# A hybrid decoder step on one core: final states, gate product, memsets and two stages of the RWKV part placed elsewhere in the order

## The chip, the cores and the metric

The kernel runs on one core of a Trainium2 chip. Five engines of the core matter here, and each runs its own instructions in order: PE (TensorE: matrix products and transposes; its weight loads are listed apart as PEld), DVE (VectorE), ACT (ScalarE), POOL (GpSimd) and SP (SyncE, which in this kernel only issues DMAs). PE writes to PSUM, which has 8 banks per partition; DVE and ACT read PSUM, POOL works in SBUF. The metric is device time in microseconds (us), the median of the runs shown; less is better.

## What is computed

One inference step of one layer, for a prompt of 512 rows and 8 samples of 8 new rows each, so 576 rows in all. The normalised input goes through one wide projection. Two branches then run side by side, RWKV-7 time mixing and differential attention; sigmoid gates merge them, and a squared-ReLU MLP with a final norm follows. The part that the change touches is the RWKV branch:

```python
def rwkv7_branch(Pr, S0, lp):
    r, k, v, wd, ad, gd = jnp.split(Pr, RWKV_SPLITS, axis=-1)
    w = -jax.nn.softplus(-(lp['w0'] + jnp.tanh(wd) @ lp['w2']).astype(f32)) - 0.5
    decay = jnp.exp(-jnp.exp(w))
    a = jax.nn.sigmoid((lp['a0'] + ad @ lp['a2']).astype(f32))
    g = jax.nn.sigmoid(gd) @ lp['g2']
    ...
    kk = kk / jnp.maximum(jnp.linalg.norm(kk, axis=-1, keepdims=True), 1e-12)
    k = k.astype(f32) * (1.0 + (a - 1.0) * lp['k_a'].astype(f32))
    S, y = rwkv7_scan(S0, hs(r), hs(decay), hs(k), hs(v), -kk, kk * hs(a))
    mean = jnp.mean(y, axis=-1, keepdims=True)
    var = jnp.mean(jnp.square(y - mean), axis=-1, keepdims=True)
    y = (y - mean) * lax.rsqrt(var + GN_EPS) * ln_x_w + ln_x_b
    bonus = jnp.sum(hs(r) * hs(k) * lp['r_k'], axis=-1, keepdims=True) * hs(v)
    o = (y + bonus).reshape(B, T, W_A).astype(Pr.dtype) * g
    return o, S
```

The state S, one 64 x 64 matrix per head, is an output too, for the prompt and for each sample.

## The kernel before

Data lie transposed: features on the 128 partitions, the 576 rows along the free axis. The recurrence is done in chunks of 64 rows: 8 chunks of the prompt, and a ninth that holds the 8 samples. The 8 RWKV heads go in four head pairs, hp 0 to 3; the two heads of a pair (`par` 0 and 1) share the partitions, 64 each.

**Dense products.** Every large projection is a generator (`stream`, L154): it loads a weight tile, ACT and DVE split it into a high and a low half (`halve`), and it then yields one matmul after another, 288 columns each. `waiting` is a list of such generators: `zs` and `shifted` (ps_z, the RWKV inputs), `gate` (ps_g) and `branch_b` (ps_brb). `take(n)` (L216) puts the next n of their matmuls at this place of the program; `fill(n)` (L224) does the same and also ties them behind the last matmul issued so far (`issue_after` gives an order on one engine, not a wait). The rest of the kernel's PE time between 190 and 525 us is the chunked recurrence, made of small products, with dense ones between them.

**The planner.** The program is not issued as written. A planner orders the instructions of each engine: of those that it holds for ready it takes the one that stands first in the program (or has a priority of its own, `prio`). So a later instruction may go ahead of an earlier one that still waits for data or for a buffer. Once the order is made, each engine keeps it, whatever the true times are.

**Buffers.** `bank(name)` gives one of three PSUM banks in turn ("w"); `tbank` and `cbank(0, ...)`, `cbank(1, ...)` give one bank each, used by the solves of stage 3, by the chain, and later by the MLP. In SBUF, the tag "G" has three tiles, shared by nb, vm, y2 and oa; a fourth tile waits until one of the three has been read for the last time.

**Stages of one head pair.** `rwkv(hp)` (L742) is a generator too, cut by `yield` into stages:

1. Norms and masks (L752 to L836): squares of k, column sums pn, the norm by a power on POOL (nr, L760), its spread to 640 columns (nb, L763), the transposes pk of nb, decays (u, cum, pe, pinv), kk, the bonus product pbn from rkp, the stacked tiles KB and ST, and the masked products pA. POOL sets the unused half of each ST to zero (L818).
2. Keys and states (L840 to L872): the transposes pV into SVU and pK into KBt, the load of the samples' states s0, and their products pI.
3. The solves (L876 to L926): eight steps pW/pZ, with 9 dense products tied behind each, and the tile TT.
4. Final states of the samples (L929 to L941): two masked copies vm on POOL, four matmuls pF, two DVE operations on sn, a store issued by POOL.
5. Mean and variance of the outputs (L944 to L955): DVE and ACT, with the tile y2 and a power on POOL (`rpow`, L240 to L243).
6. Outputs (L958 to L976): y times the power, transposes pTy, copies into oa by ACT, scale, bonus, then the gate product pg in two halves, each multiplied into oa. For hp 2 and 3, `split` (L983) makes the high and low halves (oab) for the branch product; hp 0 and 1 are stored to memory and loaded again later (L1078).

`chain(pr)` (L987) runs the nine chunks in order for two head pairs at once; it needs stages 1 to 3 of both and makes their y. `run(*stages)` (L1045) advances each named head pair by one stage. The list of calls from L1051 to L1081 is the order of the whole part:

```python
    run(0, 0)
    take(221)
    run(0, 1, 1)
    take(106)
    run(1)
    chain(0)
```

After `chain(1)` come `take(226)`, the final states of hp 2 and 3, their means and variances, and then for each of them 47 dense products and the outputs. What is left of the dense list follows (`take(2001)`), then the branch products ps_bra (L1101), which read oab of all four head pairs, and the output projection ps_wo.

Of the kernel before, what the change touches and what calls it, by code (L numbers as in the profile page):

```python
# [8 lines left out]
F32 = mybir.dt.float32  # L9
# [6 lines left out]
P = 128  # L16
# [3 lines left out]
NB = 8  # L20
# [16 lines left out]
C_ID, C_OB, C_M, C_MS, C_LM, C_I32, C_HS, C_SEL, C_MB, C_CM, C_END = (  # L37
    0, 128, 256, 384, 512, 672, 704, 706, 738, 746, 748)
# [3 lines left out]
def tile_hybrid_step(ctx, tc, xT, xsT, ktab, vtab, s0T, ptab, w_in, vecs, w2a2, g2, lamv,  # L42
                     w_bra, w_brb, w_out, w_up, w_down, cst, bias_p, bias_s,
                     yT, kTo, vTo, Sp, Ss, sh):
    nc = tc.nc
    PE, VE, AE, GE = nc.tensor, nc.vector, nc.scalar, nc.gpsimd
    PS = bass.MemoryType.PSUM

    def pool(name, bufs=1, stack=ctx, **kw):
        return stack.enter_context(tc.tile_pool(name=name, bufs=bufs, **kw))  # L50
# [6 lines left out]
    def act(out, in_, func=AF.Copy, **kw):  # L57
        ring["act"] = AE.activation(out=out, in_=in_, func=func, **kw)  # L58

    def tt(out, a, b, op, eng=None):  # L60
        ins = (eng or VE).tensor_tensor(out=out, in0=a, in1=b, op=op)  # L61
        if eng is None:
            ring["tt"] = ins

    def stt(out, a, s, b, op0, op1):
        VE.scalar_tensor_tensor(out=out, in0=a, scalar=s, in1=b, op0=op0, op1=op1)
# [4 lines left out]
    def mm(out, lhsT, rhs, start=True, stop=True):  # L71
        ring["mm"] = PE.matmul(out=out, lhsT=lhsT, rhs=rhs, start=start, stop=stop)  # L72
        return ring["mm"]
# [17 lines left out]
    MUL, ADD, SUB, MAX = ALU.mult, ALU.add, ALU.subtract, ALU.max  # L91
# [9 lines left out]
    def bank(name):  # L101
        return psw.tile([P, 512], F32, tag="w", name=name)

    def tbank(name):
        return psc.tile([P, 512], F32, tag="t", name=name)

    def cbank(i, name):
        return (psy if i else psc).tile([P, 512], F32, tag=f"c{i}", name=name)
# [3 lines left out]
    c = const.tile([P, C_END], F32, name="cst_sb")  # L112
# [103 lines left out]
    def take(n):  # L216

        while waiting and n:
            if next(waiting[0], None) is None:
                waiting.pop(0)  # L220
            else:
                n -= 1

    def fill(n):  # L224

        with tc.issue_after(ring["mm"].ins):
            take(n)
# [43 lines left out]
    with tc.tile_pool(name="xin", bufs=2, reuse_waits="tile") as xin:  # L271
# [6 lines left out]
        for k in range(0, KT, 4):  # L278
            for j in range(3):
                with prio(FEED + 1000 + 10 * k + j):  # L280
                    name = f"raw_{'qkv'[j]}0_{k}"
                    if k == 0:
                        raw = ring["pool"].tile([P, 4, P], F32, tag="raw", name=name, bufs=3)
                    else:
                        raw = zw.tile([P, 1 + NX], F32, tag="z" if j else "tz", name=name,
                                      bufs=2 if j else 1)[:, :4 * P].rearrange("p (k w) -> p k w", k=4)
# [378 lines left out]
    for h in range(HB):  # L665
        if h:
            qkv(h)
        for cc in range(2):
            GE.tensor_copy(
                out=qbd[64 * cc:64 * cc + 64, :, h, 8 * cc:8 * cc + 8],  # L670
                in_=qT[64 * cc:64 * cc + 64, h, NPR:].rearrange("p (b q) -> p b q", b=NB))
# [45 lines left out]
    rt = pool("rt", 2, stack=rk, reuse_waits="tile")  # L717

    def ch(a):
        return a.rearrange("p (c t) -> p c t", t=64)  # L720

    def m3(ap_, n):
        q, w = ap_.shape
        return ap_.rearrange("p (o w) -> p o w", o=1).broadcast_to([q, n, w])
# [14 lines left out]
    pair = {}  # L739
    halves = [(par, slice(64 * par, 64 * par + 64)) for par in range(2)]  # L740

    def rwkv(hp):  # L742
        e = hp % 2
        own = pair.setdefault(hp // 2, {})
# [3 lines left out]
        def tmp(tag, bufs=1):  # L748
            return rt.tile([P, NT], F32, tag="T", name=f"{tag}_{hp}", bufs=6)
# [5 lines left out]
        for t, o in enumerate(toks):  # L755
            mm(pn[:, 2 * t:2 * t + 2], sq[:, o:o + P], c[:, C_HS:C_HS + 2])
        (fill if hp != 2 else take)(8)
        nr = stat.tile([P, 10], F32, tag="nr", name=f"nr{hp}")
# [1 line left out]
        GE.tensor_tensor(out=nr, in0=nr, in1=mhalf[:, :10], op=ALU.pow)  # L760

        nb = rt.tile([P, 5, P], F32, tag="G", name=f"nb{hp}", bufs=3)
        GE.tensor_copy(out=nb.rearrange("p t (a d) -> p (t a) d", a=2),  # L763
                       in_=nr.rearrange("p (a o) -> p a o", o=1).broadcast_to([P, 10, 64]))
        u = tmp("u")
        aa = tmp("aa")
        for t0, n in HALF:
# [12 lines left out]
        pc = rb_.tile([P, 16], F32, tag="pc", name=f"pc{hp}", bufs=4)  # L780
# [33 lines left out]
        for par, rows in halves:  # L814
            stt(KB[rows, :, par], ch(aa)[rows], 0.5, ch(pinv)[rows], MUL, MUL)
            tt(KB[rows, :, 1 - par], ch(k2)[rows], ch(pinv)[rows], MUL)
            st = rb_.tile([P, NCH, 2, 64], F32, tag=f"ST{par}", name=f"ST{par}_{hp}")
            GE.memset(st[64 - 64 * par:128 - 64 * par], 0.0)  # L818
            stt(st[rows, :, 0], ch(kk)[rows], -1.0, ch(pm)[rows], MUL, MUL)
            tt(st[rows, :, 1], ch(r)[rows], ch(pe)[rows], MUL)  # L820
            ST.append(st)
# [4 lines left out]
        for par in range(2):  # L826
            rows = slice(64 * par, 64 * par + 64)
# [14 lines left out]
        SVU = own["SVU"][:, :, e]  # L842
        for cs, pV in two_chunks(f"pV{hp}", vv):
            for a, c0, c1 in cs:
                src = pV[64 * a:64 * a + 64].rearrange("p (c w) -> p c w", w=P)[:, :(c1 - c0 + 1) // 2]
                act(SVU[64:128, c0:c1:2, 0], src[:, :, 0:64])
                act(SVU[0:64, c0:c1:2, 1], src[:, :, 64:128])
        if hp >= 2:
            fill(8)
        KBt = rb_.tile([P, NCH, 2, 64], F32, tag="KBt", name=f"KBt{hp}")  # L850
        for c0, cn in ((0, 4), (4, 4), (8, 1)):
# [5 lines left out]

        s0 = rt.tile([P, NB, 64], F32, tag="s0", name=f"s0_{hp}")
        nc.sync.dma_start(out=s0, in_=s0T[hp])
        (fill if hp == 3 else take)(8)  # L860
        pI = bank(f"pI{hp}")
        for b in range(NB):
            for par, rows in halves:
# [2 lines left out]
        for par in range(2):  # L866
            rows = slice(64 * par, 64 * par + 64)
# [57 lines left out]

        own[e] = ST, KBt, TT, ABR, pc  # L926
        yield

        pF = bank(f"pF{hp}")  # L929
        vms = []  # L930
        for par in range(2):
            vm = rt.tile([P, NB, 64], F32, tag="G", bufs=3, name=f"vm{hp}{par}")
            tt(vm, m3(SVU[:, 8, par], NB),
               c[:, C_MB:C_MB + NB].rearrange("p (b o) -> p b o", o=1).broadcast_to([P, NB, 64]), MUL, GE)
            vms.append(vm)
        for par, rows in halves:
            mm(pF[rows], KBt[:, 8, par], vms[par].rearrange("p b i -> p (b i)"))
        sn = s0
        tt(sn, s0, pF.rearrange("p (b i) -> p b i", b=NB), ADD)
        tt(sn, sn, pc[:, 8:16].rearrange("p (b o) -> p b o", o=1).broadcast_to([P, NB, 64]), MUL)  # L940
        nc.gpsimd.dma_start(out=Ss[hp], in_=sn)  # L941

        yield
        y = own["y"][:, e]  # L944

        mean = stat.tile([P, NCH], F32, tag="mean", name=f"mean{hp}")
# [20 lines left out]
        ts(oa, oa, v(V_LW + hp), MUL, v(V_LB + hp), ADD)  # L967
        tt(oa, oa, bv, ADD)
        for t0, n in HALF:
            pg = bank(f"pg{hp}{t0}")  # L970
            mm(pg[:, :n], wg[:, hs], sg[:, t0:t0 + n])
            tt(oa[:, t0:t0 + n], oa[:, t0:t0 + n], pg[:, :n], MUL)
            if hp >= 2:
                split(oab[hp], oa, t0, n)
        if hp < 2:
            nc.gpsimd.dma_start(out=oa_d[hp], in_=oa)  # L976

    oab = [None] * 4

    def half_rows(hp):  # L980
        oab[hp] = rb_.tile([P, 2, NT], F32R, tag=f"ST{hp % 2}", name=f"oab{hp}")

    def split(dst, src, t0, n):  # L983
        act(dst[:, 0, t0:t0 + n], src[:, t0:t0 + n])
        tt(dst[:, 1, t0:t0 + n], src[:, t0:t0 + n], f32(dst[:, 0, t0:t0 + n]), SUB)
# [55 lines left out]


    gens = [rwkv(hp) for hp in range(4)]

    def run(*stages):  # L1045
        for hp in stages:
            while Pt[8 + hp] is None:
                take(2)
            next(gens[hp], None)
# [3 lines left out]
    waiting += ga[:5]  # L1053
    run(0, 0)
    take(221)
    run(0, 1, 1)
    take(106)
    run(1)
    chain(0)
    run(2, 0, 1)  # L1060
    take(190)
# [6 lines left out]
    run(0, 1)  # L1068
    chain(1)
    take(226)  # L1070
    run(2, 3, 2, 3)
    for hp in range(2, 4):
        with tc.issue_after(ring["mm"].ins):
            take(47)
            run(hp)
    for hp in range(2):
        o_ = rt.tile([P, NT], F32, tag="T", name=f"oa{hp}", bufs=6)
        nc.sync.dma_start(out=o_, in_=oa_d[hp])  # L1078
        half_rows(hp)
        split(oab[hp], o_, 0, NT)  # L1080
# [216 lines left out]
    rows = []  # L1297
    for d, n in enumerate((None, "t1", "b11", "t2", "b21", "t3", "b22", "t4")):
        if n:
            t = fp.tile([P, 2, 4, 288], F32R, tag=f"h_{n}", name=f"w3_{d}", bufs=1)  # L1300
            t = t.rearrange("p i k t -> p (i k t)")
# [5 lines left out]
    for t0, n in LAST:  # L1307
# [47 lines left out]
        for d in range(KT):  # L1355
# [4 lines left out]
            if d + 1 in ends:  # L1360
                i = ends.index(d + 1)
# [119 lines left out]
```

## Time and profile before

| what | us |
|---|---|
| median of 3 runs | 1008.45 (1007.78 to 1008.55) |
| the profiled execution | 1010.31 |
| its span, first to last instruction | 1008.5 |
| PE busy | 977.0 |
| DVE busy | 692.2 |
| ACT busy | 496.6 |
| POOL busy | 99.3 |

The profile is of one execution; all its times count from the start of the span. A row of the timeline has start, duration, engine, line, operation, output and inputs, shapes, and in brackets the idle time of the engine before it with what ended it. Many helpers record their operations at one line (L61, L66, L69 on DVE, L58 on ACT, L72 and L76 on PE, L150 for weight loads), so the name of the tile tells which operation it is. Matmul durations overlap, since the next one starts before the last has ended; the distance of two starts is what a matmul costs. The granted clock of PE is 1.00 at full speed; its mean over the span is 0.990.

### The profile page before, as it was taken

To read this page: it belongs to the slowest core of one execution; us is meant where nothing else is said; L and a number is where in the kernel's file an instruction comes from. 1 tells how busy PE (TensorE), PEld (TensorE's weight loads), DVE (VectorE), ACT (ScalarE), POOL (GpSimd) and SP (SyncE) were. 2 spreads that over 40 slices of the span, in tenths; PEclk is the share of its full clock that TensorE was granted. 3 is DMA by queue.
4 is the path that set the end of the run, shared out by engine and by line. 5 is a ranking of instruction groups with operands and counts; after the bars stand their busy time and mean duration, and the time that the engine had idled before them with its cause. 6 is when DMAs were issued, how large, how long until landed. Compare 5 with 4: busy or idle time off the path is not lost.

```text
span 1008.5 us, 24415 instructions
## 1 busy us (share of the span) xinstructions
PE 977.0 (97%) x10012; PEld 920.4 (91%) x10012; DVE 692.2 (69%) x1445; ACT 496.6 (49%) x1086; POOL 99.3 (10%) x179
## 2 busy tenths in 40 slices
PE   9999999899999998999989999999999999999996
PEld 9999998898888887988879999999999999999996
DVE  6698666864937679454569888966666666666744
ACT  6576555344435354453334656644444444444732
POOL 2511001301010430000210120000000000000001
PEclk9999999999989999999999999999999999999998
DMA  7322673121121135323366632222222222221402
GB/s 266 138 66 88 203 223 120 50 65 45 43 68 45 59 109 156 97 80 113 102 203 203 211 121 87 88 90 90 89 85 92 86 85 84 85 84 43 134 3 94
DMA packets 50833, 105.75 MB, mean 105 GB/s; under 512 B 6066, under 2 KB 8114, under 8 KB 50594
## 3 DMA queue, kind: packets, MB, share of 16 engines
q1 hardware_dynamic: 47442, 96.95, 30.0%
q0 software_dynamic: 1648, 5.35, 1.5%
q8 instruction: 79, 1.29, 0.6%
q10 hardware_dynamic: 1632, 1.89, 0.5%
q14 instruction: 32, 0.26, 0.1%
HBM read 89.38 MB, written 14.78 MB: 103 GB/s over the span
## 4 chain that ended last, share of the span: by engine, by line
PE 81%; DVE 8%; ACT 5%; issue 3%; POOL 1%; DMA 1%; DVEq 0%; SPq 0%; POOLq 0%; ACTq 0%
PE ps_dn L72 20%; PE ps_g L72 9%; PE ps_z L72 8%; PE ua L1217 5%; PE ux L1217 5%; PE ps_k L72 3%; PE ps_bra L72 2%; PE uc L1217 2%; PE ud L1217 2%; PE ub L1217 2%; PE ps_q L72 2%; PE pch L72 2%; PE ps_brb L72 2%; PE ps_v L72 2%; PE pA L72 2%
## 5 line engine op out<-in xcount | busy, mean ns | idle before, releaser
L72 PE MATMUL ps_dn<-q,hi_dn 128*128 128x288 f32 x768 | 154.8, 296 | 0.0
L72 PEld LDWEIGHTS ps_dn<-q,hi_dn 128*128 128x128 f32 x768 | 122.8, 188 | 1.4
L72 PE MATMUL ps_dn<-q,lo_dn 128*128 128x288 f32 x384 | 113.2, 295 | 0.0
L72 PE MATMUL ps_g<-xl,hi_g 128*128 128x288 f32 x256 | 80.0, 313 | 0.0
L72 PE MATMUL ps_g<-xh,lo_g 128*128 128x288 f32 x256 | 79.3, 310 | 0.7 <-issue 0.7
L72 PE MATMUL ps_g<-xh,hi_g 128*128 128x288 f32 x256 | 79.4, 310 | 0.0
L72 PEld LDWEIGHTS ps_dn<-q,lo_dn 128*128 128x128 f32 x384 | 72.0, 188 | 0.0
L72 PE MATMUL ps_z<-xh,lo_z 128*128 128x288 f32 (+1 forms) x224 | 68.9, 308 | 0.0
L72 PE MATMUL ps_z<-xh,hi_z 128*128 128x288 f32 (+1 forms) x224 | 67.6, 302 | 0.0
L72 PE MATMUL ps_z<-xl,hi_z 128*128 128x288 f32 (+1 forms) x224 | 66.9, 298 | 0.0
L61 DVE TENSOR_TENSOR ya<-ya,ps_dn 128x288 f32<-128x288 f32 x96 | 43.4, 452 | 29.4 <-PE ps_dn L72 29.4
L58 ACT ACTIVATE hi_dn<-raw_dn 128x512 fp32r<-128x512 f32 x48 | 30.1, 627 | 56.1 <-PE ps_dn L72 56.1
L1217 PE MATMUL ua<-h_b,hi 128*128 128x288 f32 x256 | 53.3, 298 | 0.9 <-ACT p L58 0.9
L72 PEld LDWEIGHTS ps_g<-xh,hi_g 128*128 128x128 f32 x256 | 49.0, 191 | 3.8 <-issue 2.6
L1217 PE MATMUL ux<-h_t,hi 128*128 128x288 f32 x256 | 52.3, 296 | 0.0
L58 ACT ACTIVATE c<-c 128x288 f32<-128x288 f32 x112 | 48.5, 439 | 6.5 <-DVE c L61 4.9
L72 PEld LDWEIGHTS ps_g<-xl,hi_g 128*128 128x128 f32 x256 | 48.9, 191 | 1.9
L72 PEld LDWEIGHTS ps_g<-xh,lo_g 128*128 128x128 f32 x256 | 48.9, 191 | 1.6 <-DVE lo_g L61 0.2
L58 ACT ACTIVATE hi<-a 128x1024 fp32r<-128x1024 f32 (+1 forms) x32 | 27.0, 845 | 43.0 <-PE ps_dn L72 34.9
L61 DVE TENSOR_TENSOR lo<-s,hi 128x1024 fp32r<-128x1024 f32 x32 | 39.2, 1225 | 10.5 <-ACT hi L58 10.4
L72 PE MATMUL ps_dn<-q,w 128*128 128x320 f32 (+1 forms) x336 | 46.3, 297 | 0.0
L72 PEld LDWEIGHTS ps_dn<-q,w 128*128 128x128 f32 x336 | 45.2, 190 | 0.1
(399 smaller groups left out, 2816.9 us busy)
## 6 DMA issues: line engine op xcount, KB each, us to landing
a<-in_w_up_dram SPq DMA_DIRECT2D x32, 512.0 KB, 3.3
raw_dn<-in_w_down_dram SPq DMA_DIRECT2D x64, 256.0 KB, 2.9
raw_g<-in_w_in_dram SPq DMA_DIRECT2D x32, 256.0 KB, 3.1
raw_z<-in_w_in_dram SPq DMA_DIRECT2D x28, 256.0 KB, 2.9
gt_d<-gg SPq DMA_DIRECT2D x16, 288.0 KB, 2.4
g<-gt_d SPq DMA_DIRECT2D x16, 288.0 KB, 3.5
kp<-in_ktab_dram SPq DMA_DIRECT2D x16, 256.0 KB, 3.9
vp<-in_vtab_dram SPq DMA_DIRECT2D x16, 256.0 KB, 3.5
```

The costliest lines, as they stand in the source:

```text
L58: ring["act"] = AE.activation(out=out, in_=in_, func=func, **kw)
L61: ins = (eng or VE).tensor_tensor(out=out, in0=a, in1=b, op=op)
L72: ring["mm"] = PE.matmul(out=out, lhsT=lhsT, rhs=rhs, start=start, stop=stop)
L1217: ring["mm"] = PE.matmul(out=ps[:, :288], lhsT=l[:, k], rhs=hb[blk][:, h, k], start=start and i == 0, stop=i == 11, skip_group_check=skip)
```

## The change

Four edits, all of order or place; the arithmetic is the same.

- The final states become a function. hp 0 and 1 call it where stage 4 was; for hp 2 and 3 it becomes the last stage, behind the outputs.
- The gate product pg of hp 2 and 3 uses `tbank` and `cbank(0)` for its two halves, not two of the three "w" banks.
- The memsets of ST are tied, on POOL, behind the spread of the norm (nb) of the same head pair.
- Stage 2 of hp 1 comes behind `take(106)`, with 8 dense products tied behind its pV (new) and 8 tied behind its pK (before: 8, not tied).

```diff
+    def final_states(hp, SVU, KBt, s0, pc):
+
+        pF = bank(f"pF{hp}")
+        vms = []
+        for par in range(2):
+            vm = rt.tile([P, NB, 64], F32, tag="G", bufs=3, name=f"vm{hp}{par}")
+            tt(vm, m3(SVU[:, 8, par], NB),
+               c[:, C_MB:C_MB + NB].rearrange("p (b o) -> p b o", o=1).broadcast_to([P, NB, 64]), MUL, GE)
+            vms.append(vm)
+        for par, rows in halves:
+            mm(pF[rows], KBt[:, 8, par], vms[par].rearrange("p b i -> p (b i)"))
+        sn = s0
+        tt(sn, s0, pF.rearrange("p (b i) -> p b i", b=NB), ADD)
+        tt(sn, sn, pc[:, 8:16].rearrange("p (b o) -> p b o", o=1).broadcast_to([P, NB, 64]), MUL)
+        nc.gpsimd.dma_start(out=Ss[hp], in_=sn)
+
     def rwkv(hp):
...
-        GE.tensor_copy(out=nb.rearrange("p t (a d) -> p (t a) d", a=2),
-                       in_=nr.rearrange("p (a o) -> p a o", o=1).broadcast_to([P, 10, 64]))
+        spread_ = GE.tensor_copy(out=nb.rearrange("p t (a d) -> p (t a) d", a=2),
+                                 in_=nr.rearrange("p (a o) -> p a o", o=1).broadcast_to([P, 10, 64]))
...
-            GE.memset(st[64 - 64 * par:128 - 64 * par], 0.0)
+            with tc.issue_after(spread_.ins):
+                GE.memset(st[64 - 64 * par:128 - 64 * par], 0.0)
...
-        if hp >= 2:
+        if hp >= 1:
             fill(8)
...
-        (fill if hp == 3 else take)(8)
+        (fill if hp % 2 else take)(8)
...
         own[e] = ST, KBt, TT, ABR, pc
         yield
-
-        pF = bank(f"pF{hp}")
...
-        nc.gpsimd.dma_start(out=Ss[hp], in_=sn)
-
-        yield
+        if hp < 2:
+            final_states(hp, SVU, KBt, s0, pc)
+            yield
         y = own["y"][:, e]
...
         for t0, n in HALF:
-            pg = bank(f"pg{hp}{t0}")
+
+            pg = bank(f"pg{hp}{t0}") if hp < 2 else cbank(0, f"pg{hp}{t0}") if t0 else tbank(f"pg{hp}{t0}")
             mm(pg[:, :n], wg[:, hs], sg[:, t0:t0 + n])
...
         if hp < 2:
             nc.gpsimd.dma_start(out=oa_d[hp], in_=oa)
+        else:
+            yield
+            final_states(hp, SVU, KBt, s0, pc)
...
     take(221)
-    run(0, 1, 1)
+    run(0, 1)
     take(106)
-    run(1)
+    run(1, 1)
     chain(0)
...
     take(226)
-    run(2, 3, 2, 3)
+    run(2, 3)
     for hp in range(2, 4):
         with tc.issue_after(ring["mm"].ins):
             take(47)
             run(hp)
+    run(2, 3)
```

More of the change, by code (lines that the diff above doesn't have):

```diff
@@ L927, in rwkv @@
         yield
-        pF = bank(f"pF{hp}")
[L930 to L940, printed above, removed]
-        nc.gpsimd.dma_start(out=Ss[hp], in_=sn)
-        yield
+        if hp < 2:
+            final_states(hp, SVU, KBt, s0, pc)
+            yield
         y = own["y"][:, e]
```

## The prediction

> **What bounds the kernel now.** I read the page's busy times first, then the waits of PE between 165 and 560 us (where the changed stages run), then PE's clock in stretches around the longest of these waits.
>
> ```profile
> PE 977.0 (97%) x10012; PEld 920.4 (91%) x10012; DVE 692.2 (69%) x1445; ACT 496.6 (49%) x1086; POOL 99.3 (10%) x179
> ```
> ```profile
> PE pk L76 <- POOL nb L763: 2.7, 1, 2.7
> PE pbn L72 <- DVE rkp L66: 2.7, 3, 1.8
> PE pg L72 <- ACT oa L58: 1.5, 2, 1.1
> PE pI L72 <- ACT KBt L58: 1.3, 3, 0.8
> PE pTy L76 <- DVE y L61: 1.2, 1, 1.2
> ...
> PE pK L76 <- ACT SVU L58: 0.4, 1, 0.4
> ...
> PE pF L72 <- POOL vm L61: 0.3, 1, 0.3
> ```
> ```profile
> 272.42:275.84 3.42, 2.17 (x34) 1.75 (x34) 2.56 (x8) 3.29 (x10) 0.00 (x0) 1.00 0.00 0
> 275.84:279.26 3.42, 3.42 (x27) 3.24 (x26) 2.11 (x7) 1.42 (x5) 0.19 (x1) 0.50 0.00 0
> 279.26:282.67 3.41, 3.41 (x81) 2.73 (x80) 0.95 (x1) 0.91 (x2) 2.48 (x2) 0.50 0.02 5
> 385.08:388.49 3.41, 3.41 (x81) 3.07 (x80) 3.13 (x5) 1.78 (x3) 0.00 (x0) 0.50 0.82 251
> 511.37:514.78 3.41, 3.01 (x10) 2.73 (x11) 2.42 (x5) 0.79 (x3) 0.92 (x1) 0.50 0.62 168
> ```
>
> PE is busy for 977.0 of 1008.5 us, so nothing but PE's idle 31.5 us and its slow stretches can be won; the change removes no product. In the table of waits the columns are the sum, the number and the longest; the rows that the change can reach, pbn aside, add to 2.7 + 1.5 + 1.3 + 1.2 + 0.4 + 0.3 = 7.4 us. The windows (length, busy time of PE, weight loads, DVE, ACT and POOL, then the granted clock) show a second price: after a stretch in which PE was busy for only 2.17 of 3.42 us, the clock stands at 0.50 for 6.83 us. Two more stretches of 3.41 us at 0.50 lie behind the longest pbn wait and behind the pTy and pg waits. So a wait of 1 to 2 us can cost its own length and, here, up to 1.7 us more for each slow stretch.
>
> **Norms of hp 0: memsets behind the power.**
>
> ```profile
> 175.84 0.80 POOL L711 DMA_DIRECT2D ob_d<-obs  x1 [1.34 <-DVE nr L69]
> 176.68 2.16 POOL L818 MEMSET ST<- 64x1152 f32 x2
> 178.82 2.19 POOL L760 TENSOR_TENSOR nr<-nr,mhalf 128x10 f32<-128x10 f32 x1
> ```
> ```profile
> 181.25 0.71 POOL L763 COPY nb<-nr 128x640 f32<-128x640 f32 x1
> ```
> ```profile
> 179.03 0.29 PE L72 MATMUL ps_z<-xh,lo_z 128*128 128x296 f32 x1
> 182.01 0.66 PE L76 MATMUL pk<-cst_sb,nb 128*128 128x128 f32 x4 [2.68 <-POOL nb L763]
> ```
>
> The two memsets (2.14 us from their start to the power's) stand between the power and its input, which DVE had ready before the store of L711 was issued. With them behind nb, pk could start at 182.01 - 2.14 = 179.87, against a PE whose dense work ends at 179.3. But other small POOL jobs that are free to go (state copies and TT memsets, now behind the power) can slip into the gap, since the planner takes what is ready. The gain lies between 0.7 (some 1.4 us of such jobs) and 2.1 us; I take **-1.6**, nearer to the full shift. What is late next is rkp for pbn, on DVE; that chain hangs on pk and moves along. Behind the memsets POOL now holds SVU copies and TT memsets, which only the next stages want. For hp 1 and hp 2 the memsets come behind their own powers too, and the mask products that read them stay behind DVE's chain from those powers; I cost that at nothing, and 2.1 us if this cover failed.
>
> A price for new neighbours is in the trace: a tiny copy on DVE took seven times its usual time beside hp 1's memsets.
>
> ```profile
> 183.48 2.17 POOL L818 MEMSET ST<- 64x1152 f32 x2
> ```
> ```profile
> L782 DVE COPY pc<-pe x4: 165/166/1129, 183.4 to 375.6; 128x8 f32<-128x8 f32 x4
> ```
>
> Those memsets leave this spot, and hp 0's will be done when pc is due: nothing, or 1 us either way. [...]
>
> **Memsets of hp 3.** Before, they ran ahead of hp 3's norms, among the final states of hp 0 and 1. Now they come behind its nb:
>
> ```profile
> 368.40 0.71 POOL L763 COPY nb<-nr 128x640 f32<-128x640 f32 x1
> 369.56 3.56 POOL L243 TENSOR_TENSOR var<-var,mhalf 128x9 f32<-128x9 f32 x2 [0.45 <-DVE var L69]
> ```
> ```profile
> 371.39 0.76 DVE L61 TENSOR_TENSOR y<-y,var 128x576 f32<-128x576 f32 x1 [1.78 <-POOL var L243]
> ```
>
> By order they go ahead of the powers of the variances of hp 0 and 1, which then start 2.1 us later. DVE's queue stands at y behind the first of these, and behind y stand u, cum and the chain to rkp and pbn. If y keeps its place, pbn is 2.1 us later. If y falls behind u, the chain starts up to 1.8 us earlier, the longest pbn wait goes, and the slow stretch at 385 with it (up to 1.7 us): -3.4. The signs differ and no row decides; I take **0**, ends +2.1 and -3.4.
>
> **Keys and states of hp 1 behind 106 dense products.**
>
> ```profile
> 275.19 1.37 PE L72 MATMUL pI<-ST,s 64*64 64x16 f32 x32 [0.81 <-ACT KBt L58]
> 276.49 2.29 PE L72 MATMUL pn<-cst_sb,sq 128*128 128x2 f32 x10
> ```
> ```profile
> 173.88 1.28 PE L72 MATMUL pn<-cst_sb,sq 128*128 128x2 f32 x10
> ```
> ```profile
> 552.01 6.26 PE ps_wo L72 x47
> ```
>
> pK waits 0.43 us for SVU and pI 0.81 for KBt, 1.24 together, with no dense product at hand: the 106 were spent while DVE made rkp and the masked tiles. The new order ties 8 products behind the last pV and 8 behind the last pK. At 6.26 / 47 = 0.133 us each, eight make 1.07 us, more than either wait. But only 8 are additional; the other 8 were free before and filled the mask stage, which can idle for 1.07 us in their place. So idle time gains 1.24 - 1.07 = 0.17. The clock is the larger part: pn took 2.29 us at half clock against 1.28, 44% lost. Of the 6.83 slow us, 0.65 belong to pI, bound by its 32 issues; 44% of 6.18 is 2.7. With 16 products in the stretch that was busy for 2.17 of 3.42 us I expect the clock to stay at 1.00. **-2.9** in all; ends 0 and -4.7 (1.24 + 3.4). The chain behind keeps its groups of 9 products, and the 8 that are spent here are missing only from the remainder behind the last outputs.
>
> **Tail of hp 2 and 3: final states behind the outputs, pg in own banks.**
>
> ```profile
> 487.01 3.37 POOL L61 TENSOR_TENSOR vm<-SVU,cst_sb 128x512 f32<-128x512 f32 x3 [0.96 <-DVE SVU L1011]
> ```
> ```profile
> 506.74 1.83 POOL L243 TENSOR_TENSOR var<-var,mhalf 128x9 f32<-128x9 f32 x1
> ```
> ```profile
> 498.43 1.93 PE L72 MATMUL pF<-vm,KBt 128*64 128x512 f32 x6
> ```
> ```profile
> 509.42 0.76 PE L76 MATMUL pTy<-cst_sb,y 128*128 128x128 f32 x5 [1.20 <-DVE y L61]
> ```
> ```profile
> 520.01 0.71 PE L76 MATMUL pTy<-cst_sb,y 128*128 128x128 f32 x5
> ```
> ```profile
> 527.31 0.40 PE L72 MATMUL ps_bra<-oab,hi_bra 128*128 128x288 f32 x1 [0.69 <-DVE oab L61]
> ```
> ```profile
> L61 DVE TENSOR_TENSOR s<-s,pF x2: 679/684/689, 499.6 to 503.4; 128x512 f32<-128x512 f32 x2
> ```
> ```profile
> 525.00:550.00 25.00, 23.88 (x176) 23.42 (x177) 22.56 (x52) 10.92 (x24) 0.00 (x0) 1.00 0.74 235
> ```
>
> Three vm fill the three "G" tiles at 487; the squares y2 need one and so wait for pF, which reads vm, and the variance's power waits on POOL behind the two state stores until 506.74. That is why pTy waits at 509. With the states at the end the power follows the sums directly, many us before PE asks for pTy: -1.20; pF's own wait: -0.33. pg waited 1.10 + 0.39 us for a bank that ACT was still reading; in two banks that are idle since the chain it waits for nothing: -1.49. The slow stretch at 511 follows these waits and lost half of its 3.01 busy us: -1.5. Together -4.5.
>
> Against it, four vm (3.37 us for three), eight pF (1.93 us for six), four s on DVE (0.68 each, 2.7 in all) and two stores on POOL's queue move into the time from hp 3's pTy to the full run of branch products, 520.01 to 527.31, whose last wait is for DVE. PE's pF only change place, and stand in for the eight dense products missing there. vm of hp 3 needs a "G" tile that oa or an earlier vm has left; I allow 0.5 us for PE waiting there and 0.5 for an s ahead of a split, with ends 0 and 9 (rival d). In the branch stage DVE is busy for 22.56 of 25 us and could take an s or two. **-3.5**.
>
> **Sum.** -1.6 + 0 - 2.9 - 3.5 = -8.0 us from the profiled execution of 1010.31 us (span 1008.5, 1.8 around it): 1002.3. That execution is 1.86 above the median, so the median goes from 1008.45 to 1000.4, rounded down.
>
> **Rivals.** (a) The half clock does not hang on these waits and stays: 2.7 + 1.5 are not won, 1004.6. For it: the longest wait, 2.68 us before 182, has no slow stretch behind it. Against: all three slow stretches lie right behind waits. Chance 0.15. [...]
>
> (b) y keeps its place behind the later power: 1000.4 + 2.1, and one more half-clock stretch at 385, 1.7: 1004.2. For it, DVE runs in order and stood there before. Chance 0.15. (c) y falls back: 1000.4 - 3.4 = 997.0. For it, other DVE work is at hand at once. Chance 0.10.
>
> (d) **Slower:** the final states stand ahead of the branch products, by pF on PE's queue or by s on DVE's. One hp takes two vm (2.2), two pF pairs (1.3), two s (1.4): 4.9; both in a row 9.8, less the 0.7 that was waited there anyway: 9.1. With a slow stretch kept (1.7) the tail is -3.0 + 9.1 + 1.7 = +7.8 and the whole -1.6 - 2.9 + 7.8 = +3.3: 1011.7. It crosses over once the stall passes 5.8 us. Against it: vm of hp 2 needs no late tile, and POOL is idle then. Chance 0.08.
>
> (e) It does not do what it says, because the planner takes what is ready and the stages come out much as before: 1007.5. Chance 0.07.
>
> **Numbers.** The forecast, 998 to 1003, has 0.45. The range, 996 to 1006, holds it and (a), (b), (c), and leaves out (d) and (e), 0.15. A measurement of this kernel can tell about 0.2%, 2 us, from no change; faster by more than that has 0.84, within it 0.09 (mostly e), slower 0.07 (d).
>
> **What would show it.** hp 0's pk waits less than 1.5 us; no clock of 0.50 around 273 to 283; pTy and pg of hp 2 without a wait and no 0.50 near 510; the pbn wait of hp 3 tells (b) from (c); pF lies between hp 3's pTy and the full run of branch products, which starts some 4 us nearer to the chain's end than now. I would be wrong with a new wait of over 2 us on pF or ps_bra, or with as many slow stretches as now.

## The result: slower, and the profile after

| what | before | after |
|---|---|---|
| median, us | 1008.55 (5 runs, 1007.78 to 1011.96) | 1019.59 (5 runs, 1016.12 to 1021.45) |
| ratio | | 1.0091, interval 1.0075 to 1.0107 |
| the profiled execution, us | 1010.31 | 1017.1 |
| its span, us | 1008.5 | 1015.3 |

The ratio says 9.2 us (7.6 to 10.8) of 1008.55, the medians of five runs 11.0; the prediction was 1000.4, with a range that ended at 1006. The profiled executions lie 6.8 us apart, so the traces show that much of it. Below, the price of an edit is its ratio's distance from 1, times before's median.

First the line of busy times after, then the table of PE's waits between 165 and 560 us, which is to be laid beside the one in the prediction (sum, number, longest).

```profile
PE 975.7 (96%) x10012; PEld 919.9 (91%) x10012; DVE 697.3 (69%) x1445; ACT 496.1 (49%) x1086; POOL 100.8 (10%) x179
```
```profile
PE pk L76 <- POOL nb L779: 3.9, 1, 3.9
PE ps_brb L72 <- DVE gg L61: 3.2, 1, 3.2
PE pbn L72 <- DVE rkp L66: 2.8, 2, 1.6
PE ps_g L72 <- DVE gg L61: 2.5, 1, 2.5
PE pA L72 <- DVE ST L61: 2.3, 1, 2.3
PE ps_bra L72 <- DVE oab L61: 1.8, 1, 1.8
```

PE does the same 10012 products in about the same busy time (977.0 before), so the loss of this execution is waiting. The waits that the change was to remove are gone: pTy and pg stand nowhere in the full table, and at hp 1 neither pK nor pI waits (0.43 and 0.81 before). But pk waits longer (2.7 before), and three waits of over 2 us are new: ps_brb, ps_g and pA. Each of the four leads to a place where the order of POOL or DVE, or what runs beside what, is not what I took it to be.

**hp 0's norm.** POOL's timeline after, around the power:

```profile
176.06 0.25 POOL L888 COPY SVU<-cst_sb 64x64 f32<-64x64 f32 x1
...
178.47 1.20 POOL L888 COPY SVU<-cst_sb 64x64 f32<-64x64 f32 x1
...
179.84 1.99 POOL L776 TENSOR_TENSOR nr<-nr,mhalf 128x10 f32<-128x10 f32 x1
181.89 0.72 POOL L779 COPY nb<-nr 128x640 f32<-128x640 f32 x1
182.67 2.16 POOL L835 MEMSET ST<- 64x1152 f32 x2
```

The memsets do stand behind nb. In the place that they left, twelve small jobs ran (state copies, state memsets, TT memsets), 176.06 to 179.84, 3.8 us where the memsets had taken 2.1.

**hp 3's norm.** POOL and DVE after:

```profile
374.16 0.83 POOL L779 COPY nb<-nr 128x640 f32<-128x640 f32 x1
375.05 2.16 POOL L835 MEMSET ST<- 64x1152 f32 x2
377.18 1.79 POOL L243 TENSOR_TENSOR var<-var,mhalf 128x9 f32<-128x9 f32 x1
```
```profile
379.01 0.76 DVE L61 TENSOR_TENSOR y<-y,var 128x576 f32<-128x576 f32 x1 [3.99 <-POOL var L243]
379.68 0.45 DVE L69 TENSOR_SCALAR u<-u 128x576 f32<-128x576 f32 x1
...
383.64 0.45 DVE L61 TENSOR_TENSOR gg<-ps_g,R 128x288 f32<-128x288 f32 x1
```

DVE stood 3.99 us at y (1.78 before), and behind y in its queue stand u and, as the ninth, the evacuation gg of a PSUM bank (its copy out, which frees it), for which PE's ps_g waits 2.5 us. This is rival (b). Before, that gg stood second behind y (y at 371.39, gg at 372.44), so the wait is not the memsets' alone.

**hp 1's norm.** hp 1's memsets now follow its nb as well, and there they meet hp 1's u on DVE. The next rows are of the kernel with the memset edit alone, POOL, then DVE and PE:

```profile
249.31 2.17 POOL L819 MEMSET ST<- 64x1152 f32 x2
```
```profile
250.66 1.12 DVE L69 TENSOR_SCALAR u<-u 128x576 f32<-128x576 f32 x1 [1.99 <-ACT u L58]
```
```profile
263.60 1.24 PE L72 MATMUL pbn<-rkp,cst_sb 128*128 128x288 f32 x4 [1.26 <-DVE rkp L66]
```

The same two, DVE and PE, in before:

```profile
248.09 0.46 DVE L69 TENSOR_SCALAR u<-u 128x576 f32<-128x576 f32 x1 [2.00 <-ACT u L58]
```
```profile
260.37 1.24 PE L72 MATMUL pbn<-rkp,cst_sb 128*128 128x288 f32 x4 [0.62 <-DVE rkp L66]
```

So u takes 0.66 us longer, and the pbn behind it waits 0.64 longer. In the whole change u takes 1.11 us there and pbn waits 1.25.

**The masked copies of hp 0 and 1**, at 345 us, DVE and then POOL after:

```profile
345.19 3.88 DVE L61 TENSOR_TENSOR ST<-P,pe 64x576 f32<-64x576 f32 x1
```
```profile
345.40 3.04 POOL L61 TENSOR_TENSOR vm<-SVU,cst_sb 128x512 f32<-128x512 f32 x3
```

The same two in before, DVE's row of the timeline and POOL's:

```profile
345.03 0.76 DVE L61 TENSOR_TENSOR ST<-P,pe 64x576 f32<-64x576 f32 x1
```
```profile
345.16 3.54 POOL L61 TENSOR_TENSOR vm<-SVU,cst_sb 128x512 f32<-128x512 f32 x3
```

The product took 0.76 us, and POOL was held (3.54 us for three vm, 3.04 after). Now, beside three vm in a row on POOL, DVE's product takes 3.88 us; pA waits 2.3 us for it. I had not listed this place at all.

**The tail.** DVE and POOL after:

```profile
501.21 0.76 DVE L61 TENSOR_TENSOR y<-y,var 128x576 f32<-128x576 f32 x1 [1.73 <-POOL var L243]
...
505.12 1.59 DVE L61 TENSOR_TENSOR y<-y,var 128x576 f32<-128x576 f32 x1 [1.91 <-POOL var L243]
...
507.23 0.44 DVE L61 TENSOR_TENSOR gg<-ps_g,R 128x288 f32<-128x288 f32 x1
```
```profile
498.97 2.21 POOL L243 TENSOR_TENSOR var<-var,mhalf 128x9 f32<-128x9 f32 x1 [7.28 <-DVE var L69]
503.29 1.80 POOL L243 TENSOR_TENSOR var<-var,mhalf 128x9 f32<-128x9 f32 x1 [2.11 <-DVE var L69]
```

The powers do come early, at 498.97 where the first stood at 506.74. But y comes early with them: in DVE's order it now stands right behind the mean, so DVE stands 1.73 and 1.91 us for POOL's power, with an evacuation gg behind each y. The second y also takes 1.59 us for 0.76, beside a vm of the moved final states (POOL, 505.05, 1.04 us). PE asked for pTy only at 513.7, without a wait; for the bank of the second gg it asked at 504.5, and waited 3.2 us.

### The profile page after: what moved, and what is told of

The parts are those of the page before. It is cut to its first block, busy times and chain, and to the rows that moved or that the text cites. A ratio compares the mean times of both kernels' runs of the same rounds, so it can differ in the third digit from the quotient of the medians.

```text
span 1015.3 us, 24420 instructions
## 1 busy us (share of the span) xinstructions
PE 975.7 (96%) x10012; PEld 919.9 (91%) x10012; DVE 697.3 (69%) x1445; ACT 496.1 (49%) x1086; POOL 100.8 (10%) x179
## 4 chain that ended last, share of the span: by engine, by line
PE 78%; DVE 10%; ACT 4%; issue 3%; POOL 2%; DMA 2%; SPq 0%; DVEq 0%; POOLq 0%; ACTq 0%
PE ps_dn L72 20%; PE ps_g L72 8%; PE ps_z L72 7%; PE ua L1226 5%; PE ux L1226 5%; PE ps_bra L72 3%; PE uc L1226 3%; PE ub L1226 2%; PE ps_k L72 2%; PE ud L1226 2%; PE ps_brb L72 2%; PE pch L72 2%; PE ps_q L72 2%; PE ps_v L72 2%; PE pY L72 1%
```

## The experiments

Three series follow, each on a chip of its own and beside runs of the kernel before on that chip; ratios are to those, and kernels of different series are compared by their ratios.

### Each edit alone

```diff
 a_memset: the ST memsets tied behind nb, nothing else
 a_keys:   take(106) ahead of stage 2 of hp 1, fill(8) and fill(8), nothing else
 a_pg:     pg of hp 2 and 3 in tbank and cbank(0), nothing else
 a_states: final_states of hp 2 and 3 behind the outputs, nothing else
```

> Only the memsets are tied behind nb. Theory (order): the loss comes from engines that stand in line. On POOL, state copies and TT memsets go ahead of hp 0's power in place of the ST memsets (pk wait of hp 0 some 3.9 us in place of 2.7), hp 3's memsets make the variance's power late (y stalls DVE for 4.0 in place of 1.8 us), and vm of hp 0 and 1 meets DVE's ST operations (4.55 us for two in place of 1.43): +4 to +6 us over the kernel before. Rival (tail): the loss sits behind the second chain, in the moved final states; then this kernel is within 2 us of the kernel before. Rival (planner): no edit has a price of its own and the sum depends on all four; then the four single edits do not add up to +9.

> Only the keys and states of hp 1 behind the 106 products, with the fills. Theory (order): -1.5 to -3 us, as the kernel after gains about 1.7 us between hp 1's pbn and its first pW, by one half-clock stretch in place of two and by the waits of pK and pI. Rival (planner): a new order further on costs as much or more: 0 or above.

> Only pg of hp 2 and 3 in own banks. All theories: the two pg waits of 1.10 and 0.39 us go and nothing else changes place much: -1 to -1.5 us, and perhaps 1.5 more if the half-clock stretch at 511 goes.

> Only the final states of hp 2 and 3 behind their outputs. Theory (order): pTy's wait (1.2) goes, but DVE stands at y for the two powers on POOL with the evacuation of the dense products behind it (PE waits 3.2 us at ps_brb), and s and vm lengthen the way to oab (1.8 in place of 0.7): +1 to +4 us. Rival (tail): nearly all of the loss is here, +6 to +10 us.

| alone | median, us (before 1009.31) | ratio | interval | price, us |
|---|---|---|---|---|
| memsets | 1014.13 | 1.0047 | 1.0032 to 1.0062 | +4.7 |
| keys and states of hp 1 | 1012.70 | 1.0032 | 1.0017 to 1.0047 | +3.2 |
| pg banks | 1008.85 | 0.9990 | 0.9977 to 1.0004 | -1.0 |
| final states | 1013.22 | 1.0032 | 1.0016 to 1.0047 | +3.2 |

4.7 + 3.2 - 1.0 + 3.2 = 10.1 us, and the whole change costs 9.2. So the edits add up within their intervals, and three of four lose, each by a like amount. My expectation for the keys, a gain of 1.5 to 3 us, missed; the other three held. The loss does not sit in the tail alone, and it is not a price of the planner's new order as a whole.

Three of the four large waits belong to one edit each. With the memsets alone PE's order is that of before, and pk waits 3.9 us. The ps_g wait of 2.5 us stands in none of the four; with the memsets alone, where gg keeps its place close behind y, it is 0.6:

```profile
PE ps_g L72 <- DVE gg L61: 0.6, 1, 0.6
```

With the keys alone pA waits 2.3 us, behind this pair on DVE and POOL:

```profile
343.22 3.86 DVE L61 TENSOR_TENSOR ST<-P,pe 64x576 f32<-64x576 f32 x1
```
```profile
343.42 3.04 POOL L61 TENSOR_TENSOR vm<-SVU,cst_sb 128x512 f32<-128x512 f32 x3
```

The profiled execution of that kernel is the fastest of its ten and takes 1010.35 us, as before's did, with 6.8 us at half clock where before's had 13.7. So it shows the wait, and not the whole loss. With the states alone PE's row at the tail is that of the whole change:

```profile
501.83 0.85 PE L72 MATMUL ps_brb<-obh,hi_brb 128*128 128x288 f32 x2 [3.19 <-DVE gg L61]
```

From 501 us on the clock stands at 0.50 for 6.8 us.

The pg edit gains some 1.0 us, where its waits were 1.5 long and a slow stretch was charged to them, and its interval holds no change too. In its trace pg waits no more, but two waits for DVE's gb are in the list that before did not have:

```profile
PE ps_brb L72 <- DVE gb L66: 0.8, 1, 0.8
PE ps_bra L72 <- DVE gb L66: 0.8, 1, 0.8
```

### The memsets: which of the places, and the term as it was meant

m_hp0 keeps the tie for hp 0 only. m_best does so too, and also ties the small jobs of hp 0 and 1 behind nb, so that the power is really the next job on POOL. In both, PE's order is that of before.

```diff
+with (tc.issue_after(spread_.ins) if hp == 0 else ExitStack()):
     GE.memset(st[64 - 64 * par:128 - 64 * par], 0.0)
...
+with (tc.issue_after(spread_.ins) if hp < 2 else ExitStack()):   # m_best alone
     GE.tensor_copy(out=SVU[rows, 8, par], ...)
     GE.memset(SVU[rows, 0, par], 0.0)
...
+with (tc.issue_after(spread_.ins) if hp < 2 else ExitStack()):   # m_best alone
     GE.memset(TT[b0, 8:, 32:64], 0.0)
     GE.memset(TT[b1, :, 0:32], 0.0)
```

> The memset tie for head pair 0 only; hp 1 to 3 untied as before, so hp 3's memsets stand again ahead of the variance powers' place they had before. If the loss of the memset edit (4.8 us) comes from both places (hp 0: POOL puts state copies, state memsets and TT memsets in the gap, so pk waits 3.9 us in place of 2.7 and a half-clock stretch follows; hp 3: y waits 4 us behind the later power): 1.5 to 3.5 us above before, and 1.5 to 3 us below the whole edit; hp 3's y waits 1.8 us again and no wait over 2 us is left at its pbn. If hp 3's memsets carry all of it: same as before. If hp 0's carry all of it: 4.8 above before.

> As the kernel before, but with the norm's power of hp 0 really next on POOL: its ST memsets, and the state copies, state memsets and TT memsets of hp 0 and 1, are all tied behind nb. My term of the prediction, tested as it was meant: pk starts 2 us earlier and waits 0.4 to 1.0 us in place of 2.7; 1.5 to 2.5 us below before. Rival: the wait only moves to pbn, because DVE's chain to rkp is what is late: pbn's wait of hp 0 grows by about what pk's loses, and the time is that of before within 1 us.

Measured (before 1008.14): m_hp0 1010.24, ratio 1.0020 (1.0004 to 1.0035), so +2.0 us; m_best 1006.68, 0.9983 (0.9970 to 0.9995), so -1.7. Of the 4.7 us, 2.0 belong to hp 0, and the rest, some 2.7 by the two ratios, to the ties of hp 1, 2 and 3 together; none of these was tried alone. The traces of a_memset and m_hp0, with one order on PE, show three places: pbn of hp 1 waits 1.26 us for 0.61, pA waits 0.3 for none (DVE's product takes 1.64 us for 0.75 beside a vm), and ps_g of hp 3 waits 0.6 for none. That is some 1.5 us, and the two profiled executions lie 1.5 apart. So hp 3 carries the smaller part of what can be seen. With the small jobs out of the way hp 0's tie gains what my term said (-1.6). It misses my expectation of pk's wait, 0.4 to 1.0: the wait is 1.4, for a reason that POOL's and DVE's rows of m_best show.

```profile
176.04 2.20 POOL L760 TENSOR_TENSOR nr<-nr,mhalf 128x10 f32<-128x10 f32 x1
178.30 1.80 POOL L763 COPY nb<-nr 128x640 f32<-128x640 f32 x1
```
```profile
178.23 1.36 DVE L777 TENSOR_TENSOR_SCAN cum<-reset,u 128x576 f32<-128x576 f32 x1
```

The power starts where I put it, but nb takes 1.80 us (0.71 before), now that it runs beside DVE's scan (1.36 us). The rival, that the wait only moves to hp 0's pbn, does not hold: that one does not wait (0.2 before).

### The collision of the masked copies

Before, three ST memsets stood ahead of vm, with the keys edit two. k_shield is the keys edit with one more such memset for hp 2, meant to stand ahead of vm.

```diff
+for _ in range(2 if hp == 2 and par == 1 else 1):
     GE.memset(st[64 - 64 * par:128 - 64 * par], 0.0)
```

> The edit of keys and states alone, with one more memset (1.05 us, the same zeros again) on POOL ahead of hp 2's masked state copies vm. Theory: the loss of that edit is one collision, DVE's product ST<-P,pe running 3.9 us in place of 0.75 while POOL's first vm reads SBUF, because a memset that used to hold POOL back moved away. Then ST<-P,pe takes less than 2.2 us here, pA's wait falls from 2.3 to under 0.8, and the time is 1.5 to 3 us below the edit alone (1.0032 of before): same as before or up to 1 us below. Rival: the loss lies in the order of the products on PE (fewer dense ones later); then the time stays 3 us above before though the wait is gone.

```profile
343.79 2.63 DVE L61 TENSOR_TENSOR ST<-P,pe 64x576 f32<-64x576 f32 x1
```
```profile
344.00 1.03 POOL L61 TENSOR_TENSOR vm<-SVU,cst_sb 128x512 f32<-128x512 f32 x1
344.99 1.05 POOL L819 MEMSET ST<- 64x1152 f32 x1
346.00 2.32 POOL L61 TENSOR_TENSOR vm<-SVU,cst_sb 128x512 f32<-128x512 f32 x2
```

Measured (before 1008.14): 1008.65, ratio 1.0007 (0.9992 to 1.0022), where the edit alone has 1.0032. The planner put the memset between the vm, so DVE was held for one vm and the memset and not for three vm: 2.63 us, 1.2 less than 3.86, and pA's wait fell from 2.3 to 1.1. Both are above what I expected (under 2.2 and under 0.8), so the collision is only half mended here. PE's order is that of a_keys. The time fell by 2.5 us against the edit alone, by the two ratios, of which the shorter wait explains 1.2; the two intervals overlap by little (1.0017 to 1.0022). So work added on POOL made the kernel faster, as the collision theory says. The rival of a price in PE's order is not needed for the loss against before, though it may hold for the gain that is missing (below).

### The tail with y behind the evacuations

s_ytie is the states edit with y of hp 2 and 3 put behind the last product on DVE ahead of it in the program (`ring["dve"]`; the lines that keep it are left out). PE's order is that of a_states.

```diff
+with tc.issue_after(ring["dve"].ins) if hp >= 2 else ExitStack():
     tt(y, y, b9(var), MUL)
```

> The edit of the final states alone, with the two products y times power of hp 2 and 3 put behind the evacuations that stood behind them in DVE's queue. Theory: that edit's loss comes from DVE standing at y (1.7 and 1.9 us) for the powers, with the bank evacuation that PE's ps_brb wants behind it (wait 3.2 us). Then the ps_brb wait falls under 1 us, and the time is 2 to 3 us below the edit alone (1.0032 of before): 0 to 1 us above before. Rival: the loss lies at the end of the tail, where vm and s meet oa and the splits (ps_bra's wait for oab 1.6 us, 0.7 before): then the time falls by less than 1 us and ps_bra still waits.

Measured (before 1008.14): 1008.05, ratio 0.9995 (0.9980 to 1.0011), against 1.0032 without the tie: some 3.7 us less, a little more than expected. DVE's rows show the evacuation gg ahead of the first y, and no stand at y:

```profile
497.78 0.46 DVE L61 TENSOR_TENSOR gg<-ps_g,R 128x288 f32<-128x288 f32 x1 [0.37 <-PE ps_g L72]
...
499.35 0.75 DVE L61 TENSOR_TENSOR y<-y,var 128x576 f32<-128x576 f32 x1
```

ps_brb has no wait on gg left. The rival has a part too: ps_bra still waits 1.6 us for oab, 0.7 before. That takes back most of pTy's 1.2 us, and the edit, even so, gains nothing that can be told from no change.

### All three repairs in the changed kernel, and the best of both

fix_all is the changed kernel with the ties of m_best (so the ST memsets of hp 1 to 3 are untied again), the memset of k_shield and the y of s_ytie. best_pg is the kernel before with m_best's ties and the pg banks. best_tail adds the states edit and s_ytie's tie to that. best_y4 is best_pg with y of all four head pairs tied in that way.

> The changed kernel with the three repairs together and nothing undone that the change meant: its ST memsets stay behind nb for hp 0 only, with the state and TT jobs of hp 0 and 1 behind nb too; one more memset ahead of hp 2's masked copies; the two late y behind the evacuations. Theory: the change's loss is three orders of POOL and DVE, each with its own price. Sum of the edits with repair: -1.5 (memsets) + 0.5 (keys) - 0.1 (states) - 0.5 (pg banks) = -1.6 us against before: 0.9965 to 1.0 of it, some 12 us below the changed kernel. Rival: part of the loss comes from the edits meeting each other or from the places of PE's products, which the repairs leave as the change has them: then it stays over 2 us above before.

> The two parts that gained, together and on the kernel before: the repaired memset ties (0.9983 alone) and the gate product in its own banks (0.999 alone). If they add up: 0.997 to 0.998 of before, -2 to -3 us; pk waits 1.4 us, pg does not wait.

> As the one with the two gaining parts, and the final states of hp 2 and 3 behind the outputs, with y behind the evacuations. My tail term as it was meant: pTy, pg and ps_brb without a wait of 1 us. If that pays (pTy 1.2 us, and the slow stretch that follows): 1 to 2.5 us below the one with two parts, 0.995 to 0.9965 of before. Rival: what is won at pTy is given back at ps_bra, which waits for oab 1.6 us in place of 0.7, and by two masked copies that run beside DVE's work on oa: within 1 us of the one with two parts.

> As the one with two parts, and y of all four head pairs put behind the work that stood behind it in DVE's queue, so u, cum and the chain to hp 3's rkp go ahead of y of hp 0: my rival (c). If DVE's place at y is what makes hp 3's pbn late: its wait of 1.1 to 1.8 us goes, and 1 to 3 us are won against the one with two parts. If only the wait moves (y of hp 0 and 1 late for their pTy, or the evacuations later): within 1 us of it or above. PE's order changes too (187 rows), so a difference under 2 us is no verdict on y alone.

| (before 1009.06) | median, us | ratio | interval |
|---|---|---|---|
| fix_all | 1007.28 | 0.9976 | 0.9965 to 0.9986 |
| best_pg | 1006.41 | 0.9982 | 0.9967 to 0.9996 |
| best_tail | 1005.25 | 0.9968 | 0.9955 to 0.9981 |
| best_y4 | 1006.85 | 0.9976 | 0.9962 to 0.9990 |

fix_all answers the main question. The banks and stages are where the change put them, and only 11 of PE's 10012 products stand elsewhere in its order; some jobs of POOL and two y of DVE stand elsewhere too, and the time falls from 1.0091 to 0.9976 of before. The prices add up here too: -1.7 (m_best) + 0.7 (k_shield) - 0.5 (s_ytie) - 1.0 (pg) = -2.5, measured -2.4. So the change's loss lies in those orders of POOL and DVE, the memset ties of hp 1 to 3 among them. best_pg, at -1.8 us, falls a little short of the 2 to 3 that I expected.

best_tail is the fastest kernel here, some 3.2 us under before. It misses my range by a little (0.9965), and against best_pg it is 1.4 us by the ratios, with intervals that overlap. Its waits of PE show the tail of the prediction (no pTy, no pg, no ps_brb), with one wait left there, ps_bra:

```profile
PE ps_bra L72 <- DVE oab L61: 1.8, 1, 1.8
```

best_y4 shows that rival (c) was no gain to be had: hp 3's pbn wait falls to 0.4 us (1.5 in best_pg), a pZ of the solves behind it then waits 1.8 us, and the time is within 1 us of best_pg's.

## Why the prediction was wrong, step by step

The forecast of -8.0 us became +9.2. Three of its four terms turned into losses, each because jobs of POOL or DVE came out in another order, or beside other jobs, than the term took for granted.

**Norms of hp 0, -1.6: wrong, +2.0.** The step that failed is the bound on the jobs that slip into the gap. I named them, and allowed them 1.4 us. All twelve slipped in, and they took 3.8 us, since one state copy took 1.20 us. The wait grew by 1.2 us and a slow stretch came behind it (below). With the gap kept free the term came out at -1.7.

**Memsets of hp 1, 2 and 3, 0 (ends for hp 3 +2.1 and -3.4): together some +2.7.** Two steps failed. "I cost that at nothing" for hp 1 and hp 2: the cost came not through the mask products, for which I had allowed 2.1 us, but through u: hp 1's memsets met it on DVE, and pbn waited 0.6 us longer. A price of this kind was before me, in pc beside the same memsets (1129 ns for 166), and I noted that they leave that spot, not that they meet u at the new one. At hp 3, u now comes behind the memsets and takes its usual time (0.45 us). At hp 3 the value between the two ends failed: rival (b) is what happened, y kept its place and stood for the later power. It reached PE by a way that I had not listed, the evacuation gg behind y: 0.6 us with the memsets alone and 2.5 in the whole change, while the longest pbn wait stayed at 1.8 with the memsets alone and is 1.6 in the whole change.

**Keys and states of hp 1, -2.9: the gain is there at its place and is lost two stages later, +3.2 in all.** PE's first outputs of chain(0), before and with the keys alone:

```profile
304.51 0.45 PE L72 MATMUL pY<-SVU,ABR 64*64 64x64 f32 x8
```
```profile
301.73 0.45 PE L72 MATMUL pY<-SVU,ABR 64*64 64x64 f32 x8
```

That is 2.8 us earlier, some 1.7 of it, as an estimate, by the clock (6.8 us at 0.50 there before, 3.4 with the keys alone). The step that failed is one that I put at nothing: stages that come sooner or in another order also move POOL's jobs against DVE's, and vm met DVE's product at 343 us. The collision costs PE 2.3 us of waiting, of which k_shield leaves 1.1. The local gain is not seen at the end even so (+0.7 with the collision half mended). A row of the waits between 165 and 560 us, of before and of k_shield, names a candidate, issue waits in the solves:

```profile
PE pZ L72 <- issue: 0.3, 1, 0.3
```
```profile
PE pZ L72 <- issue: 3.3, 4, 1.0
```

That the dense products spent earlier are missing there would explain it, but the same row reads 1.7 us in m_hp0, which has all of before's products in before's order:

```profile
PE pZ L72 <- issue: 1.7, 3, 0.7
```

So these waits vary without that, and where the rest of the gain went stays open.

**Tail, -3.5: +3.2 for the states and -1.0 for the banks.** The removals went as predicted: pTy of hp 2 and both pg without a wait. The size of the cost held: ps_bra waits 1.8 us for 0.7, about the 1.0 that I allowed. The step that failed is "the power follows the sums directly": it does, and takes y with it to a place in DVE's queue where nothing is free to wait 1.8 us. I priced the wait at the instruction that was moved (pTy) and not the wait at its new place. The final states themselves, rival (d), were a small part: a vm held the second y for some 0.8 us of the 3.2, and with y moved and nothing else, the edit costs nothing that can be told from no change. (The sum of rival (d) counts 1.7 us too many: its -3.0 had already left out the gain of the slow stretch, so that a stretch that is kept adds nothing. It should have read +1.6 and 1010.0.)

**The clock, -4.2 of the -8.0.** Before, 13.7 us between 165 and 560 were at 0.50, four times 3.41. After there are four again; these are their windows (length, busy time of PE, weight loads, DVE, ACT and POOL, then the clock):

```profile
182.07:185.48 3.41, 2.82 (x12) 2.82 (x13) 1.67 (x5) 0.00 (x0) 2.64 (x3) 0.51 0.00 0
281.06:284.47 3.41, 3.41 (x83) 3.07 (x82) 0.56 (x2) 0.15 (x1) 2.12 (x2) 0.51 0.21 69
352.79:356.20 3.41, 3.41 (x18) 3.41 (x17) 2.72 (x6) 1.17 (x3) 0.00 (x0) 0.50 0.00 0
533.66:537.07 3.41, 3.41 (x17) 3.41 (x16) 1.67 (x4) 0.96 (x2) 0.52 (x1) 0.50 0.68 234
```

So in these two executions rival (a) holds in the sum, though at other places. Over all runs it was worse than that: the mean granted clock is 0.989 in the five runs of the changed kernel and 0.992 in the 81 runs of before in the three series. As an estimate, a clock of c over the span costs up to (1 - c) times the span, some 11.2 us and 7.5 to 8.2, so that some 3 us of the 9.2 would be clock.

The next windows lie behind the same wait for pk, in the keys edit and then in k_shield:

```profile
182.30:185.70 3.40, 3.40 (x28) 3.40 (x27) 3.00 (x8) 1.65 (x3) 3.08 (x8) 1.00 0.00 0
```
```profile
182.30:185.70 3.40, 3.40 (x17) 3.40 (x16) 2.89 (x7) 1.83 (x3) 3.16 (x8) 0.53 0.00 0
```

The wait is 2.7 us in both. In one execution no slow stretch follows, and in the other one does, 17 products where the first has 28. The 14 traces of this case all have this place. With pk's wait at 3.9 us a slow stretch follows in three of three, with 2.7 us in two of six, and with 1.4 us in none of five. So a slow stretch cannot be charged to one wait from one execution, as I did three times; the longer wait only makes it more likely. What decides it where the wait is 2.7 us was not shown.

**What was right:** which waits would go, rival (b)'s mechanism, and that other jobs might slip into the gap. Of the two signs of being wrong, one came true, as many slow stretches as before. The other was a new wait of over 2 us on pF or ps_bra; the new ones of over 2 us came on ps_brb, ps_g and pA.

## What to carry to other kernels

When an operation is moved ahead in an in-order queue, list what stands behind it at its *new* place and who waits for that; here two stands of under 2 us at y made a wait of 3.2, more than the 1.2 that was removed. A tie behind something does not reserve the gap in front: ask which ready jobs will fill it, and tie those too. And after any shift of a stage, look at which POOL jobs now run beside which DVE operations, even where neither was edited.

## What the runs showed of the hardware

- A DVE product of two SBUF tiles (64 x 576, 0.76 us in before) takes 3.86 us with the keys alone and 3.88 in the whole change beside three vm on POOL, and u, with one tensor input, 1.12 us with the memsets alone for 0.46 before, beside POOL's memsets. It goes the other way too: beside DVE's scan, a POOL copy takes 1.80 us in m_best for 0.71 before (nb), and 1.20 in the whole change where the first of its kind takes 0.25 (SVU). So it can be either engine that is held; by what was not shown.
- Which engine is held goes with small differences of the starts. Before, vm starts 0.13 us behind the product (345.16) and POOL is held; with the keys edit it starts 0.20 us behind (343.22 and 343.42) and DVE is held, for all three. In the 14 traces POOL is held in the nine where vm starts 0.11 to 0.13 us behind, and DVE in the four where it starts 0.20 or 0.21 behind (and for one vm in a_memset, where vm starts 0.02 ahead). By the records the product was first in these thirteen, so being first does not decide it here; what does was not settled.
- In k_shield DVE stayed held across a POOL memset, which has no input: the first vm ends at 345.03, the memset behind it at 346.04, and the product at 346.42. Beside memsets with no vm ahead of them the same kind of product took its usual time (before, 342.41, 0.74 us).
- POOL's power on 128 x 9 or 128 x 10 values takes 1.8 to 2.2 us, and DVE's y stood 1.63 to 1.91 us for it in four places (before at 371 and 508, after at 501 and 505).
